# Queries, and the second half of receptances and values, as pairs of products with seven products in some chunk pairs

## The chip, the cores and the metric

The kernel runs on one core of one Trainium2 chip. The metric is the device time of one execution in microseconds, as the median of several runs. Matrix products run on TensorE (PE; its weight loads are PEld), elementwise work on VectorE (DVE), ScalarE (ACT) and GpSimd (POOL), and weights are fetched by DMA, issued from SyncE (SP).

## What is computed

One decoder layer in float32 on 256 tokens of width 2048: a feed-forward, a mixer (sliding-window attention beside an RWKV-7 recurrence, both gated), a cross attention into a memory of 256 rows, a second feed-forward, a final norm. Cut to what matters here:

```python
def gated_parallel_mixer(x, norm_g, w_in, ...):
    h = rms_norm(x, norm_g)
    p = h @ w_in                                  # 2048 x 8992
    q, k, v, p_rwkv, gates = jnp.split(p, ...)    # 1024, 256, 256, 3360, 4096 columns
    y_attn = sliding_window_attention(q, k, v, sinks)
    y_rwkv = rwkv7_time_mix(p_rwkv, ...)          # r, k, v (1024 columns each), decay, rate, gate
    gate_attn, gate_rwkv = jnp.split(jax.nn.sigmoid(gates), 2, axis=-1)
    merged = gate_attn * (y_attn @ w_proj_attn) + gate_rwkv * (y_rwkv @ w_proj_rwkv)
    return x + merged @ w_out
```

The queries are the first 1024 columns of `p`; receptances `r`, keys `k` and values `v` of the RWKV half are 1024 columns each, which the kernel takes in two halves of 512 columns, h=0 and h=1 (eight heads each).

## The kernel before

**Products.** A float32 product is made of three matmuls on numbers that were split into a high part (`hi`, rounded to TensorE's reduced float32) and the rest (`lo`): hi·hi, hi·lo, lo·hi (`times`, L470). The high part is a cast on ACT (L396), the low part a subtraction on DVE (L397). A weight comes in *units* of two chunks of 128 rows by 512 columns (half a megabyte). `weight_plan` lists all products in order, `units` and `items` are made from it, and `next_item` (L432) fetches the loads of the next units, has them split (`divide`, L408) one or two items ahead, and gives out the current one. `product` (L451) takes 16 chunks of rows, one unit at a time, for both blocks of 128 tokens: 96 matmuls for one 128x512 result each.

**Pairs with seven products.** `product_pair` (L533) computes two products with the same activations in one go, two chunks of rows by two matrices by two token blocks at a time, which is a 2x2 by 2x2 block product. A plain chunk pair takes its eight block products (24 matmuls). A chunk pair with seven takes a Strassen-like scheme of seven (21 matmuls), for which it needs four sums of weight blocks (L425 to L428), the high and low parts of those (`two_parts`, L400, names `thi` and `tlo`), and four combinations of activation blocks with their high and low parts (`combinations`, L485, lines L505 to L524). All eight PSUM banks are in use while such a chunk pair runs: `mm` and `acc` with three banks each and both banks of `tr`. The results are put together by callbacks, `first`, `middle` and `out`. Before the change only the feed-forwards use it (`gate_and_up`, `down`).

**The mixer** uses plain products. Their results leave PSUM through ACT (`scaled`, L844, scales each token by its norm factor into a tile `tok`). TensorE then transposes `tok` into features (`feat`, L654; `to_features` for queries, `shifted` for the RWKV columns). The order of products is: queries in two halves, keys with values, the small RWKV columns, RWKV keys in two halves, four attention gates alternating with `w_proj_attn`, then r and v of h=0, r and v of h=1, four RWKV gates, four of `w_proj_rwkv`, four of `w_out`, then the cross attention.

**Work beside the products** is written as generators in groups (`Interleave`): "feat" (transposes of results), "attn" (attention), "ew" (elementwise work of the recurrence: `decay_and_rate`, `removal_keys`, `substitute`, `receptances`, `values`, one at a time in this order), "chain" (`pairs(h, q)`, the recurrence itself, with many small matmuls), "norm" (`finish`, which writes the recurrence's output `yr`), "mem", and "stage". A `bg.tick()` between groups of six matmuls lets each go one step. `pairs(h, q)` waits until `substitute` and `values(h)` are done; `w_proj_rwkv` reads `yr`. `stage` prepares ten sums of weights for the second feed-forward in DRAM, starting at the items that `STAGE_AT` names. This is the order of issue in the program; the builder that turns it into the queues of the engines may move an instruction ahead of others where its inputs are there.

**Memory.** The mixer's large tiles come from one tag, `t4`, with 23 buffers of 4 KB per partition (`N4`). At its start the mixer's tiles take the place of the feed-forward's; POOL builds constants there (`mixer_constants`, L195), two of which ACT casts (L230).

## Time and profile before

| | |
|---|---|
| median of three runs | 2247.78 us (2247.43 to 2248.47) |
| the profiled execution | 2248.79 us, its span 2247.1 us |
| mean granted TensorE clock | 0.999 |
| PE busy | 2231.4 us, 99% of the span |
| PEld busy | 1833.6 us, 82% |
| DVE busy | 1820.5 us, 81% |
| ACT busy | 1245.0 us, 55% |
| POOL busy | 134.9 us, 6% |
| DMA, mean | 205 GB/s |

The profile shows one execution. Times are microseconds from the first instruction. "L397" is a line of the kernel as printed here. Busy time of PE is the union of the modelled durations of matmuls that overlap in its pipeline, so what one matmul costs is read from the distance between two starts. In a timeline a row is: start, length, engine, line, operation, output tile <- input tiles, shape, count, and in brackets the idle time before it with what ended it. In the 40 slices a digit is a busy share in tenths; a slice is 56.2 us.

### The profile page before, as it was taken

The numbers are of one execution on the slowest core, as the hardware profiler recorded it, in microseconds if no ns is written. First come the engines' busy times: TensorE is split into PE (matmuls) and PEld (weight loads), VectorE is DVE, ScalarE is ACT, GpSimd is POOL, SyncE is SP. The second block draws the span as 40 slices with busy tenths as digits, with TensorE's granted clock in tenths as the row PEclk, the third lists the DMA queues.
The fourth block names the chain that finished last, engine by engine and source line by source line (L and its number), as shares of the span: only waits on it lengthen the run. The fifth ranks groups of instructions, "written<-read, shape, count | busy, mean of one in ns | idle before, by whom it ended". The sixth has DMA issues, their size and how long they took to land.

```text
span 2247.1 us, 28239 instructions
## 1 busy us (share of the span) xinstructions
PE 2231.4 (99%) x10587; PEld 1833.6 (82%) x10587; DVE 1820.5 (81%) x2342; ACT 1245.0 (55%) x1621; POOL 134.9 (6%) x192
## 2 busy tenths in 40 slices
PE   9999999999999999999999999999999999999998
PEld 7888888888888877788888888888888888888886
DVE  7898988998989476977656666547999999999997
ACT  6555555555556567544444446456665466555654
POOL 1000000000001000201320040001000000000002
PEclk9999999999999999999999999999999999999999
DMA  7555555556556544676767576547565566556564
GB/s 264 187 201 197 201 198 202 200 188 212 195 193 201 169 135 150 198 231 207 224 214 263 187 258 227 190 167 272 197 237 204 195 231 218 201 205 221 197 229 146
DMA packets 229225, 461.35 MB, mean 205 GB/s; under 512 B 15227, under 2 KB 17504, under 8 KB 229088
## 3 DMA queue, kind: packets, MB, share of 16 engines
q1 hardware_dynamic: 220512, 433.62, 56.8%
q0 software_dynamic: 8112, 25.12, 3.5%
q8 instruction: 83, 1.36, 0.2%
q10 hardware_dynamic: 464, 0.79, 0.1%
q14 instruction: 54, 0.44, 0.1%
HBM read 435.91 MB, written 23.59 MB: 204 GB/s over the span
## 4 chain that ended last, share of the span: by engine, by line
PE 95%; DVE 2%; DMA 1%; issue 1%; ACT 1%; SPq 0%; POOL 0%; POOLq 0%; DVEq 0%; ACTq 0%
PE acc L473 19%; PE acc L474 19%; PE acc L475 19%; PE mm L475 8%; PE mm L474 8%; PE mm L473 8%; PE tr L661 2%; PE tr L474 2%; PE tr L473 2%; PE tr L475 2%; PE mm L1313 1%; DVE lo L397 1%; PE tr L1249 1%; DMA raw<-in_w_out_dram 0%; PE mm L903 0%
## 5 line engine op out<-in xcount | busy, mean ns | idle before, releaser
L396 ACT CAST hi<-raw 128x1024 fp32r<-128x1024 f32 (+1 forms) x770 | 756.5, 992 | 714.4 <-PE acc L475 514.8
L397 DVE TENSOR_TENSOR lo<-raw,hi 128x1024 fp32r<-128x1024 f32 (+1 forms) x770 | 886.1, 1153 | 315.5 <-ACT hi L396 314.0
L473 PE MATMUL acc<-hi,xhi 128*128 128x512 f32 (+1 forms) x1166 | 462.2, 397 | 2.1 <-ACT xhi L688 1.7
L474 PE MATMUL acc<-lo,xhi 128*128 128x512 f32 (+1 forms) x1166 | 452.7, 388 | 0.0
L475 PE MATMUL acc<-hi,xlo 128*128 128x512 f32 (+1 forms) x1166 | 452.5, 388 | 0.0
L473 PEld LDWEIGHTS acc<-hi,xhi 128*128 128x128 f32 x1166 | 219.4, 188 | 49.8 <-issue 4.0
L475 PEld LDWEIGHTS acc<-hi,xlo 128*128 128x128 f32 x1166 | 218.8, 188 | 46.0 <-DVE xlo L689 1.0
L474 PEld LDWEIGHTS acc<-lo,xhi 128*128 128x128 f32 x1166 | 219.2, 188 | 43.8 <-issue 1.7
L404 ACT CAST thi<-raw 128x1024 fp32r<-128x1024 f32 x192 | 199.9, 1052 | 62.9 <-DVE raw L427 42.4
L405 DVE TENSOR_TENSOR tlo<-raw,thi 128x1024 fp32r<-128x1024 f32 x192 | 232.2, 1219 | 1.1 <-ACT thi L404 0.4
L474 PE MATMUL acc<-lo,hhi 128*128 128x512 f32 x372 | 145.5, 391 | 0.8 <-DVE lo L397 0.8
L475 PE MATMUL acc<-hi,hlo 128*128 128x512 f32 x372 | 145.5, 391 | 0.0
L473 PE MATMUL mm<-hi,xhi 128*128 128x512 f32 x370 | 145.4, 393 | 0.0
L473 PE MATMUL acc<-hi,hhi 128*128 128x512 f32 x372 | 144.9, 390 | 0.0
L475 PE MATMUL mm<-hi,xlo 128*128 128x512 f32 x370 | 144.3, 390 | 0.0
L474 PE MATMUL mm<-lo,xhi 128*128 128x512 f32 x370 | 144.2, 390 | 0.0
L474 PEld LDWEIGHTS acc<-lo,hhi 128*128 128x128 f32 x372 | 69.9, 188 | 15.4 <-DVE lo L397 1.2
L473 PEld LDWEIGHTS acc<-hi,hhi 128*128 128x128 f32 x372 | 69.9, 188 | 14.3
L475 PEld LDWEIGHTS mm<-hi,xlo 128*128 128x128 f32 x370 | 69.4, 188 | 14.6
L475 PEld LDWEIGHTS acc<-hi,hlo 128*128 128x128 f32 x372 | 69.9, 188 | 14.0
L474 PEld LDWEIGHTS mm<-lo,xhi 128*128 128x128 f32 x370 | 69.5, 188 | 14.2
L473 PEld LDWEIGHTS mm<-hi,xhi 128*128 128x128 f32 x370 | 69.5, 188 | 14.0
(396 smaller groups left out, 3595.7 us busy)
## 6 DMA issues: line engine op xcount, KB each, us to landing
raw<-in_ffn_w_down_dram SPq DMA_DIRECT2D x88, 1024.0 KB, 5.1
raw<-in_ffn_w_gate_dram SPq DMA_DIRECT2D x84, 1024.0 KB, 5.1
raw<-in_ffn_w_up_dram SPq DMA_DIRECT2D x78, 1024.0 KB, 6.2
raw<-in_w_in_dram SPq DMA_DIRECT2D x136, 512.0 KB, 3.5
raw<-in_w_out_dram SPq DMA_DIRECT2D x32, 512.0 KB, 4.4
raw<-sums SPq DMA_DIRECT2D x20, 512.0 KB, 6.3
raw<-in_w_proj_attn_dram SPq DMA_DIRECT2D x16, 512.0 KB, 4.4
raw<-in_w_proj_rwkv_dram SPq DMA_DIRECT2D x16, 512.0 KB, 4.8
```

Source lines behind the costliest of these rows:

```text
L396: at["hi"] = act.copy(hi[:, s], raw[:, s])
L397: at["lo"] = dve.tensor_tensor(lo[:, s], raw[:, s], f32(hi[:, s]), ALU.subtract)
L404: act.copy(hi[:], v[:])
L405: dve.tensor_tensor(lo[:], v[:], f32(hi[:]), ALU.subtract)
L473: pe.matmul(o, xh, hi, start=first, stop=False, **how)
L474: pe.matmul(o, xh, lo, start=False, stop=False, **how)
L475: pe.matmul(o, xl, hi, start=False, stop=last, **how)
L661: pe.transpose(b[:, o : o + P], tok[:, t, col : col + P], ident[:])
L1249: pe.matmul(b[e][:, o : o + P], x1[r, j, cs_], x2[r, j, cs_], start=True, stop=True)
L1313: pe.matmul(vb[:, (o + k) * P : (o + k + 1) * P][:, r], lhs(k, e), rhs[:, k, r], start=first and k + e == 0, stop=True, **ek,)
```

## The change

The two halves of the queries become one pair of products, with seven products in chunk pairs 2, 4 and 6 of eight (counted from 0). The receptances h=1 and the values h=1 become one pair, with seven in chunk pairs 4 and 6; the order of products becomes r of h=0, v of h=0, then the pair, and `receptances(0)` is now spawned after both products of h=0. The combinations of activations are computed at the start of the mixer for pairs 2, 4 and 6 and kept for the second use. Sums of weights, their parts and the combinations take `t4` tiles there. A flag `at["sevens"]` is set from the first chunk pair with seven to the end of the last; `values` and the start of `pairs` wait while it is set. `STAGE_AT` is 16 items lower; the plan has 16 items fewer ahead of that place, since a pair of products has 8 items where two products have 16.

```diff
+SEVEN_Q, SEVEN_RV = (2, 4, 6), (4, 6)
+
-STAGE_AT = [266 + 2 * n for n in range(10)]
+STAGE_AT = [250 + 2 * n for n in range(10)]
...
-    cols = [0, 512, ATTN_W]
-    for c in cols:
-        yield w_in, 0, KD, c, 512
+    yield (w_in, w_in), 0, KD, (0, 512), SEVEN_Q
+    yield w_in, 0, KD, ATTN_W, 512
...
-    for h in range(2):
-        yield w_in, 0, KD, C_RW + h * 512, 512
-        yield w_in, 0, KD, C_RW + 2 * RW + h * 512, 512
+    for c in (C_RW, C_RW + 2 * RW):
+        yield w_in, 0, KD, c, 512
+    yield (w_in, w_in), 0, KD, (C_RW + 512, C_RW + 2 * RW + 512), SEVEN_RV
...
+    def room(name, dt=F32):
+
+        if at["pool"] is None:
+            return at["t4"](name, (P, KU, 512), dt)
+        return wp.tile([P, KU, 512], F32, tag="raw", name="raw", bufs=4)
...
     def two_parts(v, e):
         sp = at["pool"]
-        hi = sp.tile([P, KU, 512], F32R, tag="thi" + e, name="thi")
-        lo = sp.tile([P, KU, 512], F32R, tag="tlo" + e, name="tlo")
+        if sp is None:
+            hi, lo = room("thi", F32R), room("tlo", F32R)
+        else:
...
     divide:
-            t = [wp.tile([P, KU, 512], F32, tag="raw", name="raw", bufs=4) for _ in range(2)]
+            t = [room("sums") for _ in range(2)]
...
     combinations:
+                if parts:
+                    hi, lo = (p[:, o : o + n, :] for p in parts)
+                else:
+                    p = room(name, F32R)[:].rearrange("p a (b n) -> p (a b) n", n=P)
+                    hi, lo = p[:, :n], p[:, 4 : 4 + n]
...
     product_pair:
                 bg.until(lambda: c["done"] and (q > min(seven) or not bg.groups["feat"][1]))
+                at["sevens"] = True
...
                 if end:
                     middle(b)
+                    at["sevens"] = False
...
+        def scaled_pair(c, w):
+
+            s = [t4("tok", (P, 2, 512)) for _ in range(2)]
+            u = t4("u", (P, 2, 512))
+            u2, u3 = u[:, 0], u[:, 1]
+
+            def first(b):
+                act.copy(s[0][:, 0], b["p1"][:])
+                act.copy(s[1][:, 1], b["q"][:])
+
+            def middle(b):
+                dve.tensor_tensor(u2, b["p6"][:], s[0][:, 0], ALU.add)
+                dve.tensor_tensor(u3, b["p7"][:], u2, ALU.add)
+                dve.tensor_tensor(u2, b["p5"][:], u2, ALU.add)
+                dve.tensor_tensor(s[1][:, 1], s[1][:, 1], u3, ALU.add)
+
+            def out(b, to):
+                t, n = int(to in ("p4", "p5")), int(to in ("p3", "p5"))
+                o = s[n][:, t]
+                more = {"p2": o, "p4": u3, "p3": u2, "p5": o}[to]
+                dve.tensor_tensor(o, b[to][:], more, ALU.add)
+                act.activation(o, o, AF.Copy, scale=n2.r[t])
+
+            product_pair(n2.x, c, w, first, middle, out)
+            return s
...
+        cx = combinations(None, n2.x, SEVEN_Q, "c", early=False)
         qt = []
-        for h in range(2):
-            tok = scaled(product(n2.x, W["w_in"]), n2.r)
+        for tok in scaled_pair(cx, W["w_in"]):
             qt.append(t4("qt"))
-            bg.spawn("feat", to_features(tok, qt[h], "q"))
+            bg.spawn("feat", to_features(tok, qt[-1], "q"))
...
     values (twice), and pairs after its idle steps:
+                while at["sevens"]:
+                    yield
...
         for h in range(2):
             rt.append(t4("rt"))
-            columns4(rt[h], 4 * h, f"r{h}")
+            if h == 0:
+                columns4(rt[h], 4 * h, f"r{h}")
+                bv.append(t4("bv"))
+                columns4(bv[h], 16 + 4 * h, f"v{h}")
+            else:
+                bv.append(t4("bv"))
+                for tok, o, m, name in zip(scaled_pair(cx, W["w_in"]), (rt[h], bv[h]), (4, 20), "rv"):
+                    bg.spawn("feat", shifted(
+                        tok, C4, [m + i for i in range(4)], [o[:, i, :] for i in range(4)],
+                        name + "1",
+                    ))
             bg.spawn("ew", receptances(h))
-            bv.append(t4("bv"))
-            columns4(bv[h], 16 + 4 * h, f"v{h}")
             bg.spawn("ew", values(h))
```

More of the change, by code (lines that the diff above doesn't have):

```diff
@@ L319, in decoder_layer @@
             continue
+        if len(ends) == 1:
+            for q in range(nk // KU):
+                items.append(((len(units), len(units) + 1), q in n))
+                units += [(v, k0 + KU * q, c, 512) for v, c in zip(w, c0)]
+            continue
         for k in range(k0, k0 + nk, 2 * KU):
@@ L330, in decoder_layer @@
     sums_d = dram.tile([len(staged), P, 4, 512], F32, name="sums")
-    at = {"item": 0, "product": 0, "pool": None}
+    at = {"item": 0, "product": 0, "pool": None, "sevens": False}
+    def room(name, dt=F32):
+        if at["pool"] is None:
+            return at["t4"](name, (P, KU, 512), dt)
+        return wp.tile([P, KU, 512], F32, tag="raw", name="raw", bufs=4)
     def load(u, pieces=None):
@@ L401, in two_parts @@
         sp = at["pool"]
-        hi = sp.tile([P, KU, 512], F32R, tag="thi" + e, name="thi")
-        lo = sp.tile([P, KU, 512], F32R, tag="tlo" + e, name="tlo")
+        if sp is None:
+            hi, lo = room("thi", F32R), room("tlo", F32R)
+        else:
+            hi = sp.tile([P, KU, 512], F32R, tag="thi" + e, name="thi")
+            lo = sp.tile([P, KU, 512], F32R, tag="tlo" + e, name="tlo")
         act.copy(hi[:], v[:])
@@ L490, in combinations @@
         n = n or sum(4 if q in seven else 2 for q in pairs)
-        parts = [sp.tile([P, n, P], F32R, tag=name + e, name=name + e) for e in ("hi", "lo")]
-        c = {"parts": parts, "at": {}, "done": False, "seven": seven, "early": early}
+        parts = sp and [
+            sp.tile([P, n, P], F32R, tag=name + e, name=name + e) for e in ("hi", "lo")
+        ]
+        c = {"at": {}, "done": False, "seven": seven, "early": early}
         def work():
@@ L500, in work @@
                     yield
-                t = wp.tile([P, KU, 512], F32, tag="raw", name="raw", bufs=4)
+                t = room("sums")
                 v = t[:, 0].rearrange("p (k t n) -> p k t n", k=2, t=2)
@@ L518, in work @@
                 yield
[L519 removed]
+                if parts:
[3 more added lines that the diff above has]
+                    hi, lo = p[:, :n], p[:, 4 : 4 + n]
                 with tc.issue_after(at["hi"].ins):
[L521 removed]
+                    act.copy(hi, f[:, :n])
                 yield
                 with tc.issue_after(at["lo"].ins):
[L524 to L525 removed]
+                    dve.tensor_tensor(lo, f[:, :n], f32(hi), ALU.subtract)
+                c["at"][q] = hi, lo
                 o += n
@@ L556, in of_c @@
         def of_c(q, i):
-            return [p[:, c["at"][q] + i, :] for p in c["parts"]]
+            return [p[:, i, :] for p in c["at"][q]]
         def of_w(parts_, i):
@@ L1207, in values @@
             for i in (0, 2):
+                while at["sevens"]:
+                    yield
                 b = head_sums(
@@ L1271, in pairs @@
             yield from idle(4 + 4 * q)
+            while at["sevens"]:
+                yield
             ah, bh, kh, rh = at_[h], bt[h], aa[h], rt[h]
```

5 lines of the change are left out of this document (1 added, 4 removed).

## The prediction

> **What bounds the kernel now.** I read the page first (engine line, slices), then the windows over the stretches that the change rewrites, the waits, and last the timelines of PE and DVE there.
>
> ```profile
> span 2247.1 us, 28239 instructions
> ...
> PE 2231.4 (99%) x10587; PEld 1833.6 (82%) x10587; DVE 1820.5 (81%) x2342; ACT 1245.0 (55%) x1621; POOL 134.9 (6%) x192
> ...
> DVE  7898988998989476977656666547999999999997
> ```
>
> PE is the bound: 2231.4 us of 2247.1. DVE stands at eight or nine tenths in the two feed-forwards and falls to four to seven, with a single nine, in slices 14 to 28, where the mixer and the cross attention lie. That gap is what the change spends. The windows put numbers on it: a piece of the feed-forward's end, then the two halves of the queries, then the second receptances and the second values (columns: length, busy time and count of PE, weight load, DVE, ACT, POOL, then granted clock).
>
> ```profile
> 660.00:680.00 20.00, 20.00 (x89) 16.26 (x88) 19.82 (x24) 11.23 (x13) 0.00 (x0) 1.00 0.53 178
> 715.00:738.00 23.00, 23.00 (x111) 19.10 (x110) 15.71 (x23) 14.46 (x27) 6.60 (x25) 1.00 0.65 208
> 738.00:761.00 23.00, 23.00 (x107) 19.05 (x106) 10.09 (x9) 11.05 (x13) 0.00 (x0) 1.00 0.63 197
> ...
> 1063.00:1086.00 23.00, 23.00 (x107) 19.03 (x106) 11.39 (x12) 10.96 (x13) 2.31 (x4) 1.00 0.60 186
> 1086.00:1118.00 32.00, 31.49 (x177) 25.99 (x176) 23.07 (x29) 15.05 (x19) 15.67 (x22) 1.00 0.74 234
> ```
>
> PE is full in all of them. In the feed-forward, where pairs of seven products are in use already, DVE works 19.82 of 20 us and PE still does not wait: seven products in three of eight pairs is just what DVE can carry there. In the queries DVE works 25.8 of 46 us, in the receptances and values 34.5 of 55.
>
> **What is saved.** A chunk pair costs eight products of three matmuls each, or seven. Three pairs of the queries and two of the second half drop one product: 5 x 3 = 15 matmuls. Their price is the distance from start to start, not the 390 ns that one lasts:
>
> ```profile
> 715.28 0.39 PE L473 MATMUL acc<-hi,xhi 128*128 128x512 f32 x1
> ...
> 721.43 1.03 PE L661 MATMUL tr<-ident,x 128*128 128x128 f32 x8
> ...
> 727.34 0.39 PE L473 MATMUL acc<-hi,xhi 128*128 128x512 f32 x1
> ...
> 734.14 0.39 PE L473 MATMUL acc<-hi,xhi 128*128 128x512 f32 x1
> ```
>
> From 727.34 to 734.14 there are 30 starts, 0.227 us each. So 15 matmuls are 3.40 us: 2.04 in the queries, 1.36 in the second half. This is 0.15% of the time, and no other PE work goes: the transposes are the same, and the same 32 half-megabyte units of weights are fetched in another order, so DMA is left at nothing.
>
> **What is added on DVE.** The costs stand in the feed-forward's own pair of seven:
>
> ```profile
> 699.70 0.68 DVE L425 TENSOR_TENSOR raw<-raw,raw 128x512 f32<-128x512 f32 x1
> 700.30 0.68 DVE L426 TENSOR_TENSOR raw<-raw 128x512 f32<-128x512 f32 x1
> 700.90 0.68 DVE L427 TENSOR_TENSOR raw<-raw,raw 128x512 f32<-128x512 f32 x1
> 701.50 1.22 DVE L397 TENSOR_TENSOR lo<-raw,hi 128x1024 fp32r<-128x1024 f32 x1
> 702.64 0.68 DVE L428 TENSOR_TENSOR raw<-raw,raw 128x512 f32<-128x512 f32 x1
> 703.24 1.22 DVE L405 TENSOR_TENSOR tlo<-raw,thi 128x1024 fp32r<-128x1024 f32 x1
> 704.38 0.68 DVE L397 TENSOR_TENSOR lo<-raw,hi 128x512 fp32r<-128x512 f32 x1
> 704.98 1.22 DVE L405 TENSOR_TENSOR tlo<-raw,thi 128x1024 fp32r<-128x1024 f32 x1
> ```
>
> Start to start, a sum of weights takes 0.60, a full low part 1.14, a half one 0.60. A seven-pair is 4 x 0.60 + 1.14 + 0.60 + 2 x 1.14 = 6.42 us; a plain pair is two low parts, 2.28. Each seven-pair adds 4.14 us. The combinations of the activations:
>
> ```profile
> 655.10 0.68 DVE L505 TENSOR_TENSOR raw<-hhi,hlo 128x512 f32<-128x512 f32 x1
> 655.70 0.68 DVE L667 TENSOR_TENSOR hlo<-tr,hhi 128x512 fp32r<-128x512 f32 x1
> 656.30 0.28 DVE L511 TENSOR_TENSOR raw<-raw 128x128 f32<-128x128 f32 x1
> 656.50 0.28 DVE L513 TENSOR_TENSOR raw<-raw 128x128 f32<-128x128 f32 x1
> ...
> 658.91 0.68 DVE L524 TENSOR_TENSOR dlo<-raw,dhi 128x512 fp32r<-128x512 f32 x1
> 659.51 0.68 DVE L428 TENSOR_TENSOR raw<-raw,raw 128x512 f32<-128x512 f32 x1
> ```
>
> 0.60 + 4 x 0.20 + 0.60 = 2.0 us a pair, three pairs, in the queries alone (the second half reuses two of them). The end of a product pair, which was four scalings on ACT, gets four sums and four additions of a 128x512 tile on DVE, 8 x 0.60 = 4.8 us each time. ACT gets 1.5 more casts of about 1 us in each seven-pair; with 14.46 of 23 us and 11.05 of 23 busy it has room, so I cost that at nothing, covered by PE (without the cover: 1.6 us a pair).
>
> **The queries.** DVE's work there becomes 25.8 + 3 x 4.14 + 6.0 + 4.8 = 49.0 us, and PE needs only 46 - 2.0 = 44.0. Up to 2.4 us (the four last additions) can run behind PE's end, so DVE is 2.6 to 5.0 us short even if it never stands. And the work is not spread evenly:
>
> ```profile
> 715.71 1.28 DVE L634 SCALAR_TENSOR_TENSOR x<-acc,x 128x512 f32<-128x512 f32 x2
> ...
> 721.34 1.22 DVE L397 TENSOR_TENSOR lo<-raw,hi 128x1024 fp32r<-128x1024 f32 x1
> ...
> 726.26 0.17 DVE L708 TENSOR_SCALAR ms<-ms 128x2 f32<-128x2 f32 x1
> 727.00 1.23 DVE L397 TENSOR_TENSOR lo<-raw,hi 128x1024 fp32r<-128x1024 f32 x1 [0.57 <-ACT hi L396]
> 731.78 2.36 DVE L397 TENSOR_TENSOR lo<-raw,hi 128x1024 fp32r<-128x1024 f32 x2 [3.55 <-ACT hi L396]
> ```
>
> Up to 726.4 DVE still closes the feed-forward and the norm. PE has by then begun the pair of queries at 715.28; two plain pairs (48 matmuls, 10.9 us) and 16 transposes (0.1 us each by the row above) bring it to the first seven-pair at 727.8. DVE fills its small gaps with the first combination's sums (1.4 us), then has before PE can start: its low part 0.6, the next combination's sums 1.4, the weight sums 2.4, and a cast. That is 726.4 + 4.4 = 730.8, plus ACT's cast of about 1: PE waits 3 to 3.5 us at the first seven-pair. Behind it stand the other combinations (2.6 us) and two low parts ahead of the next plain pair: another 1.5 to 2 us. Later pairs then find DVE in step. Both ways give about 5; below stands 2.6 (work alone), above 7.5 if ACT's casts come late as well. No gain can come from here, since no DVE instruction goes away. I take 5.0. The pair of queries so ends about 3.0 us later than now.
>
> **The second half.** The receptances h=1 and values h=1 become one pair, two seven-pairs of which come late (fifth and seventh). DVE gets 2 x 4.14 + 4.8 = 13.1 us more on 34.5 of 55, and has room on the whole; but in the four chunk pairs where the two fall, PE takes 2 x 24 + 2 x 21 = 90 matmuls, 20.4 us, and DVE needs 2 x 6.42 + 2 x 2.28 = 17.4, beside 1.2 of the keys' low part and one or two staging sums (2.4 us each), which start 16 items earlier by number and about as far in the work. Stall from 0 to 1.5 us; I take 0.7, nearer to the feed-forward's row (99% busy, no wait). Net -0.7.
>
> While a pair of seven holds all PSUM banks, the values' transposes and the chain wait (the new checks on "sevens"). Two steps of `values(0)` and so `pairs(0, ...)` move from inside values h=1 to the first gate product, about seven ticks of six matmuls later, 7 x 6 x 0.227 = 9.5 us of PE work. Who waits: the last rows of the RWKV output.
>
> ```profile
> L667 DVE TENSOR_TENSOR yrlo<-yq,yrhi x4: 683/689/693, 1184.6 to 1273.8; 128x512 fp32r<-128x512 f32 x4
> ...
> L475 PE MATMUL acc<-hi,yrlo x64: 389/389/398, 1294.9 to 1340.6; 128*128 128x512 f32 x64
> ```
>
> The last part is ready at 1274.5 and first read at 1294: 20 us of cover, so the delay costs nothing; beyond 20 us each us would be PE's.
>
> **The sum**, on the profiled execution (2248.79 us, of which 2247.1 is span): -3.40 + 5.0 + 0.7 = +2.3, 2251.1. The median of the three runs is 1.0 lower than that execution, so I forecast 2250.1 us. Its own range, with the bounds above (2.6 to 7.5 and 0 to 1.5), is 2247.0 to 2253.4.
>
> **Rivals.** (1) *DVE keeps up.* The builder's order can put combinations and sums into gaps that I count as lost, as the feed-forward shows at 99%. Then only the saving is left: 2247.8 - 3.4 = 2244.4. Against it: 49 us of DVE work in 44. To be faster by over 0.2% (4.5 us) takes 1.1 us beyond the saving; the mixer's remaining PE idle, 0.5 us in 1086 to 1118, does not hold that.
>
> (2) *ACT blocks the first seven-pair.* The constants' casts wait for POOL:
>
> ```profile
> 726.09 0.31 POOL L198 MEMSET abias<- 128x256 f32 x1 [6.89 <-ACT junk L697]
> ...
> 730.29 0.30 ACT L230 CAST ones_r<-bdones 128x128 fp32r<-128x128 f32 x1 [3.32 <-POOL bdones L221]
> ```
>
> POOL cannot start before the norm has left the old buffer, and ACT stands 3.3 us for it; DVE's 3.55 us of idle time at 731.78 is the same wait. Today the ready weights hide it. If these two casts stay ahead of the combination's and the sums' casts, DVE loses its 3.3 us inside a stretch where it has none to lose: 5.0 becomes 8.3, and the time 2253.4, slower. It decides once DVE's backlog at 727 is over nothing, and by the walk above it is.
>
> (3) *The chain comes too late.* Two or three more `t4` tiles are held from the queries on, and each seven-pair takes six of the 23; if keys and values queue for them over 20 us in all, PE stands ahead of `w_proj_rwkv`. With 6 us beyond the cover: about 2256. For it: the delay of 9.5 us uses half of the cover.
>
> (4) *One long wait slows the clock.* If the stall at the first seven-pair is one piece, PE could come back at half rate for as long again: 3.4 us at twice 0.227 a matmul lose 1.7 us, 2251.8. The windows here show a clock of 1.00 throughout, and no wait of that length to test it. The Trainium skill, "TensorE: Matmul & The Clock Gate", Part 1, has such a rule: after an idle window of about 3.4 us the array runs at half its clock.
>
> **How the numbers follow.** Forecast 0.43, DVE keeps up 0.20, ACT blocks 0.26, late chain 0.08, clock 0.03. About 0.2% (4.5 us) is what a measurement of this kernel can tell from no change: 2243.3 to 2252.3. Slower by more: 0.07 of the forecast's own upper end, 0.22 of ACT's 0.26, 0.07 of the late chain's, 0.36. Faster by more: 0.06, from the first rival with something that I do not see. The rest, 0.58, is within. The range, 2244.0 to 2257.0, reaches from the first rival's time to the late chain's; about 0.06 lie under it and 0.1 above.
>
> **What would show it.** In the changed kernel's waits, PE `tr` or `acc` at L474/L473 should wait some 5 us on DVE (`tlo`, `lo`, the combinations) between 725 and 760, DVE should be 95% busy or more in that window, and the first kv product should end about 3 us later. PE without a wait there, with the product 2 us earlier, is the first rival; ACT's L230 with over 3 us idle and `thi` behind it, the second; PE waiting at `yrhi` or `yrlo`, the third; a granted clock below 0.95 there, the fourth. I am wrong altogether if the time moves outside these two stretches.

## The result, and the profile after

The changed kernel takes 2258.56 us (2257.97 to 2259.24, four runs); the kernel before takes 2247.7 us in the same measurement. The ratio is 1.0047, interval [1.0035, 1.006]: slower by 10.9 us, and above the forecast of 2250.1 and the upper end of its range. The profiled execution took 2259.24 us, its span is 2257.5. Lines of the code have moved by the change: the casts of weights are L408 (before L396), the low parts L409 (L397), the two constants' casts L231 (L230), the matmuls L488 to L490 (L473 to L475). New names: `sums` at L440 to L443 are the sums of weights, `thi` and `tlo` at L419 and L420 their parts, `c` at L542 and L545 the parts of the combinations. The edits of the experiments move these numbers by a few lines more.

The page's engine line after:

```profile
PE 2234.7 (99%) x10572; PEld 1833.5 (81%) x10572; DVE 1856.5 (82%) x2406; ACT 1255.3 (56%) x1638; POOL 136.5 (6%) x192
```

The 15 matmuls are gone (10587 to 10572), DVE has 36 us more work, and the share of PE still reads 99%. The page does not show where 10 us went; two tiles tell it. `vt` is copied out of PSUM when the keys-and-values product ends, the first product after the queries. `gl` is the first use of `w_proj_rwkv`, after all of the second half. Before, then after (the tiles' rows: shortest/median/longest ns, first and last start):

```profile
L889 ACT ACTIVATE vt<-acc,rs x2: 466/468/471, 783.8 to 785.1; 128x256 f32<-128x256 f32 x2
L1459 DVE TENSOR_TENSOR gl<-acc,gl x8: 679/681/683, 1305.1 to 1341.3; 128x512 f32<-128x512 f32 x8
```

```profile
L939 ACT ACTIVATE vt<-acc,rs x2: 464/466/467, 794.5 to 795.9; 128x256 f32<-128x256 f32 x2
L1523 DVE TENSOR_TENSOR gl<-acc,gl x8: 679/680/684, 1316.4 to 1352.6; 128x512 f32<-128x512 f32 x8
```

The queries begin at the same time in both (715.3 and 715.5), so 10.7 us are lost by the end of the first product behind them, and 11.3 by `gl`: the loss lies in the queries, although nine matmuls were saved there. The windows of after over the queries, which answer to the two shown of before (length; busy time and count of PE, weight load, DVE, ACT, POOL; granted clock; DMA):

```profile
715.00:738.00 23.00, 18.62 (x81) 14.24 (x80) 18.83 (x36) 13.35 (x27) 7.51 (x25) 0.87 0.38 124
738.00:761.00 23.00, 21.07 (x81) 16.07 (x80) 18.55 (x26) 10.53 (x13) 0.00 (x0) 0.90 0.52 178
```

PE, full before, now has 18.62 of 23 us and then 21.07. DVE was forecast at 95% or more and has only 82% and 81%: it was not simply short of time, it stood still as well. And the clock column reads 0.87 and 0.90 where it read 1.00. The waits of PE in this part, then those of ACT (us in total, times, the longest):

```profile
PE acc L488 <- ACT hi L408: 3.2, 1, 3.2
PE tr L488 <- ACT thi L419: 2.9, 3, 1.2
```

```profile
ACT thi L419 <- DVE sums L442: 6.5, 3, 4.4
ACT ones_r L231 <- POOL bdones L222: 4.7, 1, 4.7
```

Read together they are one chain. POOL holds ACT for 4.7 us at the constants' casts. The cast `hi` of the weights stands right behind them (731.80), and PE's longest wait, 3.2 us, ends with it. DVE's `c` waits 3.1 us for the cast behind that one; the next sums come late, and `thi` and PE's waits at `tr` follow those. The timelines of ACT and DVE show the order, with the idle time in brackets:

```profile
731.40 0.30 ACT L231 CAST ones_r<-bdones 128x128 fp32r<-128x128 f32 x1 [4.67 <-POOL bdones L222]
731.60 0.29 ACT L231 CAST ones_r<-bdmean 128x128 fp32r<-128x128 f32 x1
731.80 1.04 ACT L408 CAST hi<-raw 128x1024 fp32r<-128x1024 f32 x1
732.75 0.61 ACT L542 CAST c<-sums 128x512 fp32r<-128x512 f32 x1
...
736.13 1.04 ACT L419 CAST thi<-sums 128x1024 fp32r<-128x1024 f32 x1 [1.82 <-DVE sums L442]
```

```profile
729.65 0.68 DVE L440 TENSOR_TENSOR sums<-raw 128x512 f32<-128x512 f32 x1
733.40 0.69 DVE L545 TENSOR_TENSOR c<-sums,c 128x512 fp32r<-128x512 f32 x1 [3.06 <-ACT c L542]
...
757.25 0.69 DVE L440 TENSOR_TENSOR sums<-raw 128x512 f32<-128x512 f32 x1 [2.00 <-DMA raw<-in_w_in_dram]
```

And PE's timeline there:

```profile
729.35 0.39 PE L490 MATMUL acc<-hi,xlo 128*128 128x512 f32 x1
732.90 0.80 PE L488 MATMUL acc<-hi,xhi 128*128 128x512 f32 x1 [3.16 <-ACT hi L408]
...
735.38 0.63 PE L488 MATMUL mm<-hi,xhi 128*128 128x512 f32 x1
737.23 1.22 PE L488 MATMUL tr<-thi,c 128*128 128x512 f32 x2 [1.22 <-ACT thi L419]
738.25 0.63 PE L489 MATMUL acc<-lo,xhi 128*128 128x512 f32 x1
738.68 0.63 PE L490 MATMUL acc<-hi,xlo 128*128 128x512 f32 x1
```

From 738.25 to 738.68 two starts lie 0.43 us apart, nearly twice the 0.227 of before. Taking each distance between starts against 0.227 gives the loss in its parts: the two gaps at 729.35 and 735.38 lose 3.32 and 1.62 us; the matmuls between and behind them until 742.4, at half clock, 3.9; the second and third pair with seven 3.5 (at 750.3 0.72, at 758.8 1.26 behind the late weights of the row at 757.25, the rest in pieces). That is 12.3 of the 12.7 us that are to be explained (10.7 lost and 2.04 saved).

### The profile page after: what moved, and what is told of

The parts are those of the page before. It is cut to its first block, busy times and chain, and to the rows that moved or that the text cites. A ratio compares the mean times of both kernels' runs of the same rounds, so it can differ in the third digit from the quotient of the medians.

```text
span 2257.5 us, 28305 instructions
## 1 busy us (share of the span) xinstructions
PE 2234.7 (99%) x10572; PEld 1833.5 (81%) x10572; DVE 1856.5 (82%) x2406; ACT 1255.3 (56%) x1638; POOL 136.5 (6%) x192
## 3 DMA queue, kind: packets, MB, share of 16 engines
q8 instruction: 83, 1.36, 0.2%
## 4 chain that ended last, share of the span: by engine, by line
PE 91%; DVE 4%; issue 2%; DMA 1%; ACT 1%; POOL 0%; SPq 0%; POOLq 0%; ACTq 0%; DVEq 0%
PE acc L488 18%; PE acc L489 18%; PE acc L490 18%; PE mm L489 8%; PE mm L490 8%; PE mm L488 8%; PE tr L684 2%; PE tr L489 2%; PE tr L488 2%; PE tr L490 2%; DVE lo L409 2%; PE mm L1369 1%; PE tr L1303 1%; DMA raw<-in_w_in_dram 1%; PE mm L953 0%
## 5 line engine op out<-in xcount | busy, mean ns | idle before, releaser
L408 ACT CAST hi<-raw 128x1024 fp32r<-128x1024 f32 (+1 forms) x770 | 753.9, 989 | 706.4 <-PE acc L490 498.7
L409 DVE TENSOR_TENSOR lo<-raw,hi 128x1024 fp32r<-128x1024 f32 (+1 forms) x770 | 883.2, 1150 | 283.6 <-ACT hi L408 281.9
L488 PE MATMUL acc<-hi,xhi 128*128 128x512 f32 (+1 forms) x1105 | 439.3, 398 | 5.2 <-ACT hi L408 3.2
L489 PE MATMUL acc<-lo,xhi 128*128 128x512 f32 (+1 forms) x1105 | 430.5, 390 | 0.0
L490 PE MATMUL acc<-hi,xlo 128*128 128x512 f32 (+1 forms) x1105 | 429.9, 389 | 0.0
L488 PEld LDWEIGHTS acc<-hi,xhi 128*128 128x128 f32 x1105 | 208.6, 189 | 51.8 <-ACT hi L408 4.0
L490 PEld LDWEIGHTS acc<-hi,xlo 128*128 128x128 f32 x1105 | 208.0, 188 | 42.9 <-issue 0.3
L489 PEld LDWEIGHTS acc<-lo,xhi 128*128 128x128 f32 x1105 | 208.5, 189 | 41.9 <-issue 1.7
L420 DVE TENSOR_TENSOR tlo<-raw,thi 128x1024 fp32r<-128x1024 f32 x192 | 231.8, 1217 | 1.3 <-ACT thi L419 0.4
L419 ACT CAST thi<-raw 128x1024 fp32r<-128x1024 f32 x192 | 199.7, 1051 | 59.6 <-DVE raw L442 38.9
L488 PE MATMUL mm<-hi,xhi 128*128 128x512 f32 x401 | 157.9, 394 | 0.3 <-ACT hi L408 0.3
L490 PE MATMUL mm<-hi,xlo 128*128 128x512 f32 x401 | 156.3, 390 | 0.0
L489 PE MATMUL mm<-lo,xhi 128*128 128x512 f32 x401 | 156.3, 390 | 0.0
L490 PE MATMUL acc<-hi,hlo 128*128 128x512 f32 x372 | 145.5, 391 | 0.0
L488 PE MATMUL acc<-hi,hhi 128*128 128x512 f32 x372 | 145.0, 390 | 0.0
L488 PEld LDWEIGHTS mm<-hi,xhi 128*128 128x128 f32 x401 | 75.5, 188 | 16.0 <-ACT hi L408 0.7
L490 PEld LDWEIGHTS mm<-hi,xlo 128*128 128x128 f32 x401 | 75.3, 188 | 15.9
L488 PEld LDWEIGHTS acc<-hi,hhi 128*128 128x128 f32 x372 | 69.8, 188 | 14.4
L490 PEld LDWEIGHTS acc<-hi,hlo 128*128 128x128 f32 x372 | 69.9, 188 | 14.1
```

The lines of the kernel that those rows point to most:

```text
L408: at["hi"] = act.copy(hi[:, s], raw[:, s])
L409: at["lo"] = dve.tensor_tensor(lo[:, s], raw[:, s], f32(hi[:, s]), ALU.subtract)
L419: act.copy(hi[:], v[:])
L420: dve.tensor_tensor(lo[:], v[:], f32(hi[:]), ALU.subtract)
L488: pe.matmul(o, xh, hi, start=first, stop=False, **how)
L489: pe.matmul(o, xh, lo, start=False, stop=False, **how)
```

## The experiments

Four causes stand in that chain: DVE short of time (the forecast), ACT held by POOL (the second rival), the clock (the fourth), and late weights (not foreseen). The runs were made to tell them apart.

**Half of the change alone.** In queries_plain the second half is changed alone; the queries are two plain products again (the combinations of two chunk pairs, which the second half needs, are still built at the mixer's start, and `STAGE_AT` follows the plan):

```diff
-    yield (w_in, w_in), 0, KD, (0, 512), SEVEN_Q
-    yield w_in, 0, KD, ATTN_W, 512
+    for c in (0, 512, ATTN_W):
+        yield w_in, 0, KD, c, 512
...
-        for tok in scaled_pair(cx, W["w_in"]):
+        for h in range(2):
+            tok = scaled(product(n2.x, W["w_in"]), n2.r)
```

> The changed kernel with the queries as two plain products again (the combinations of two pairs, which the second half needs, still built at the mixer's start). Theory (all of the loss lies in the queries; the second half saves 1.4 us and gives it back): 2247.5 to 2248.5, and the queries as long as before. Rival (the second half costs too, by the chain's delay or by the tiles): over 2250.

Measured: 2249.38 us beside 2249.19 of the kernel before in the same measurement, ratio 1.0001 [0.9991, 1.001]. The theory's 2247.5 to 2248.5 is level with the 2247.7 that the kernel before took in the first measurement; here too the two are level. In rv_plain the queries are changed alone:

```diff
-    for c in (C_RW, C_RW + 2 * RW):
-        yield w_in, 0, KD, c, 512
-    yield (w_in, w_in), 0, KD, (C_RW + 512, C_RW + 2 * RW + 512), SEVEN_RV
+    for h in range(2):
+        yield w_in, 0, KD, C_RW + h * 512, 512
+        yield w_in, 0, KD, C_RW + 2 * RW + h * 512, 512
```

> The changed kernel with receptances and values of h=1 as two plain products again. Theory (the loss lies in the queries): 2257.5 to 2259, as the changed kernel. Rival (the second half costs): 2255 or less.

Measured: 2257.73 us, ratio 1.0037 [1.0024, 1.005], as the theory has it. The tiles' rows of the first and of the second:

```profile
L940 ACT ACTIVATE vt<-acc,rs x2: 464/466/467, 784.0 to 785.4; 128x256 f32<-128x256 f32 x2
L1524 DVE TENSOR_TENSOR gl<-acc,gl x8: 681/681/684, 1305.6 to 1341.8; 128x512 f32<-128x512 f32 x8
```

```profile
L939 ACT ACTIVATE vt<-acc,rs x2: 464/466/467, 792.8 to 794.1; 128x256 f32<-128x256 f32 x2
L1515 DVE TENSOR_TENSOR gl<-acc,gl x8: 679/681/683, 1314.5 to 1350.7; 128x512 f32<-128x512 f32 x8
```

The queries alone lose 9.0 us before `vt` and nearly nothing after it; the second half alone is at `gl` 0.5 us late, 0.2 of it from before `vt`. The loss is the queries', and the second half neither earns its 1.36 us nor costs more than about 0.3.

Up to `vt` rv_plain runs the same code as the changed kernel, and still its `vt` comes 1.7 us earlier. The two gaps of PE at the first pair with seven are as long in both (3.32 and 1.62 us), but the half clock lasts 6.83 us and not 10.24, so the slow starts cost 3.0 us and not 3.9, and the stalls at the later pairs cost 2.9 and not 3.5. A difference at `vt` between two single traces is uncertain by about that much.

**ACT's stop.** In casts_late the two constants' casts are issued behind the pair of queries:

```diff
-            act.copy(r[:], v[:])
-            ones_r.append(r)
+            ones_r.append((r, v))
...
+        with tc.issue_after(at["hi"].ins):
+            for r_, v_ in late_r:
+                act.copy(r_[:], v_[:])
```

> The changed kernel, with the two ACT casts of the block-diagonal constants issued behind the pair of queries instead of ahead of its first seven-pair. Theory (ACT stood 4.7 us for POOL there, PE stood over 3 us behind it, and the clock then fell to half for some 25 matmuls): the wait of 3.2 us at the first seven-pair and the clock of 0.5 both go; what is left is DVE's shortage of 2 to 5 us, so 2249 to 2252 against 2258.6. Rival (DVE is simply short of time in the queries): PE waits as long, now on DVE, and no more than 3 us are gained, 2255.5 or more.

Measured: 2256.34 us beside 2249.19 of the kernel before, ratio 1.0031 [1.0019, 1.0043], and `vt` at 790.4, 4.1 us earlier than in the changed kernel and 2.4 earlier than in rv_plain. The time itself lies in the rival's interval; the loss is 7.2 us where it was 10.9, and the two intervals of the ratio overlap a little. ACT's stop is gone from this stretch, but half and more of the expected gain did not come. What took its place (the first window, then a short one, then the row of PE's waits):

```profile
715.00:738.00 23.00, 20.24 (x89) 15.69 (x88) 21.90 (x38) 14.99 (x27) 7.72 (x25) 0.94 0.53 168
```

```profile
734.00:738.00 4.00, 3.83 (x11) 3.03 (x12) 4.00 (x5) 2.28 (x4) 0.00 (x0) 0.67 0.93 294
```

```profile
PE tr L487 <- ACT thi L418: 3.9, 3, 2.5
```

DVE is now at 21.90 of 23 us, 95%, and full at the first pair with seven; PE waits 2.5 us there for the sums and their parts, and the clock still falls. In the next 23 us DVE is at 19.61, 85%, and waits 1.7 us for weights. So ACT's stop is a cause, for 2.4 to 4.1 us at `vt` with the clock time that hung on it, and behind it stands the forecast's own cause.

**The clock.** In keep_warm eight small matmuls of constants are put ahead of the first pair with seven, so that PE has something to do in its gap:

```diff
+                if at["pool"] is None and q == 2:
+                    idle_ = mm()
+                    for _ in range(8):
+                        pe.matmul(idle_[:, :P], ones[:], ones[:], start=True, stop=True)
```

> The changed kernel, with eight matmuls of ones (128x128, float32, into an unused PSUM bank, result not read) between the second plain pair of the queries and the first seven-pair, where PE stands. Theory (the wait itself is 3.3 us and the slow clock behind it costs about 5 us more): the wait stays about as long in sum but is filled, the clock stays at 1.00 from 730 to 743, and 4 to 5.5 us are gained, about 2253.5. Rival (the clock in the records costs nothing, the slow matmuls wait for their operands): time unchanged or up to 1 us more, 2258 to 2260.

Measured: 2258.88 us, ratio 1.0041 [1.0026, 1.0056]. It failed: they ran at 727.8 to 729.5, ahead of the gap and not in it, and the clock fell all the same, at 734.4 instead of 732.1. To price the clock by itself, wait_short and wait_long give the kernel before a wait between the two halves of its queries and change nothing else: a matmul, and behind it the second half, that wait for a row of POOL operations, two (K = 1) and five (K = 4).

```diff
-            tok = scaled(product(n2.x, W["w_in"]), n2.r)
+            with tc.issue_after(hold_pe.ins) if h else nullcontext():
+                tok = scaled(product(n2.x, W["w_in"]), n2.r)
...
+            if h == 0:
+                slow = t4("slow", (P, 2, 512))
+                pool.tensor_tensor(slow[:, 0], tok[:, 0, :], tok[:, 1, :], ALU.add)
+                for i in range(K):
+                    pool.tensor_tensor(slow[:, 0], slow[:, 0], slow[:, 0], ALU.subtract)
+                bank = mm()
+                hold_pe = pe.matmul(bank[:, :P], slow[:, 0, :P], ones[:], start=True, stop=True)
```

> The kernel before, with a made wait on PE between the two halves of the queries: two GpSimd operations of about 1 us each on the first half's result, a small matmul that reads them (result not read), and the second half's matmuls behind it. PE stands 2.5 to 3.5 us. Theory (the clock falls after PE has stood for about as long as the 3.3 us seen): the clock stays at 1.00 or falls for a few matmuls only; lost is about the wait. Rival (any wait of over 2 us halves the clock for some 25 matmuls): another 5 us lost.

> As wait_short with five GpSimd operations, so PE stands 5.5 to 7 us. Theory: the clock falls to half and stays there for several microseconds after PE works again; start to start 0.43 us instead of 0.227 for 10 to 25 matmuls, so 2 to 5 us are lost beyond the wait. Rival (a halved clock only shows where the matmuls wait for operands anyway): the matmuls behind the wait start 0.227 us apart.

Measured in one execution each: 2255.07 and 2257.74 us. PE's starts leave 4.26 us and 7.62 us empty, and `vt` comes 6.7 and 9.7 us late (790.5 and 793.5 beside 783.8). The shorter wait so costs 2.4 us beyond itself, the longer one 2.1: a price that doesn't grow with the wait. For wait_short neither side came true (the clock fell, but 2.4 us were lost beyond the wait and not 5); for wait_long the theory did. Windows, with their edges laid where the clock changes, show why; wait_short, then wait_long:

```profile
737.58:740.99 3.41, 1.40 (x7) 0.82 (x5) 1.35 (x2) 2.31 (x3) 1.20 (x1) 1.00 0.76 232
740.99:744.40 3.41, 1.32 (x4) 1.22 (x5) 1.14 (x1) 0.00 (x0) 1.96 (x2) 0.50 0.51 142
744.40:747.81 3.41, 3.41 (x11) 2.72 (x11) 0.00 (x0) 0.48 (x1) 0.00 (x0) 0.50 0.23 88
```

```profile
736.80:740.21 3.41, 2.08 (x10) 1.38 (x8) 1.23 (x1) 2.44 (x4) 0.53 (x1) 1.00 0.79 238
740.21:743.62 3.41, 0.00 (x0) 0.00 (x0) 1.46 (x1) 0.33 (x1) 3.25 (x3) 1.00 0.52 148
743.62:747.03 3.41, 0.69 (x3) 0.69 (x4) 0.00 (x0) 0.00 (x0) 2.51 (x3) 0.50 0.39 139
747.03:750.44 3.41, 3.41 (x12) 2.72 (x12) 0.00 (x0) 0.00 (x0) 0.00 (x0) 0.50 0.00 0
```

The clock knows two values, 1.00 and 0.50, and stays at half for two times 3.41 us in both. In the longer one it did not fall during the first 3.41 us that hold a part of the wait (10 matmuls ran in them), but after the stretch with none. What the slow matmuls cost is set by how much of these 6.83 us lies behind the wait, 4.7 and 4.1 us, and not by the wait's length.

**The order of products.** In kv_first the keys and values come ahead of the pair of queries; kv_first_late has the casts of the constants behind the pair as well:

```diff
+    yield w_in, 0, KD, ATTN_W, 512
     yield (w_in, w_in), 0, KD, (0, 512), SEVEN_Q
-    yield w_in, 0, KD, ATTN_W, 512
```

> As kv_first_late, but with the constants' casts left where they are. Theory (a stop of 4 to 5 us on ACT hurts only where the weights are needed at once): with plain products behind it, PE waits 0 to 1 us more than in kv_first_late. Rival (the stop costs PE wherever it is): 3 us more.

> The changed kernel with the plain product for keys and values in front of the pair of queries, and the constants' casts behind that pair. The combinations, the norm's end and the constants then lie under 22 us of plain matmuls. Theory (the queries lose because DVE has the norm's end, the combinations and three seven-pairs in one stretch, and because ACT stands there): no PE wait over 0.5 us and no slow clock in the queries, which then save their 2 us; the second half gives nothing, so about 2 us under the kernel before, ratio 0.999. Rival (three seven-pairs of eight are too many for DVE and for four weight buffers also without the combinations): PE still waits 3 us or more in the queries, ratio 1.001 or more.

Measured: 2255.08 us, ratio 1.0029 [1.0017, 1.0041], and 2253.52 us, ratio 1.0024 [1.0015, 1.0033]. Neither is faster than the kernel before, though 2 us were forecast for kv_first_late. DVE is done with the feed-forward and the norm when the first pair with seven comes, and the stretch that was at 18.62, where the plain product now lies, is full again, at full clock (kv_first_late, the window and DVE's longest waits between 735 and 790):

```profile
715.00:738.00 23.00, 23.00 (x111) 19.11 (x110) 21.73 (x40) 15.85 (x28) 9.31 (x25) 1.00 0.68 206
```

```profile
DVE sums L439 <- DMA raw<-in_w_in_dram: 7.3, 3, 3.8
```

But DVE now stands 7.3 us for weights in the 55 us of the pair. A mixer's unit lives in a ring `raw` of four buffers, the units of two chunk pairs; a pair with seven keeps its four blocks until the last sum, so that the loads behind it can only start late (the feed-forward has a ring of its own, `raw2`, with twice the depth). PE lost about 1.5 us in this stretch (21.99 of 23 and 23.52 of 24 us in the two windows behind the one shown), yet `gl` starts at 1308.8, 3.7 us late. Waits that the kernel before doesn't have stand behind the queries: 1.5 us at the attention's transposes (`tr`, L998, three times, for DVE), and 1.7 us for `hi` and 0.5 for `lo` between 976 and 980, at the first product with `w_proj_attn`. Why this order brings them was not tried. kv_first takes 1.6 us more than kv_first_late, between its theory's 0 to 1 and its rival's 3: PE waits 2.6 us from 715 to 790 and not 1.4, and behind the same wait near 980 its clock falls for one stretch of 3.41 us, from 982.6, which it does not in kv_first_late.

**Late weights.** In deep, which is casts_late otherwise, the weights of the queries' pairs with seven are fetched into `t4` tiles, eight units ahead:

```diff
+        elif u in roomy and at["pool"] is None:
+            raw = at["t4"]("rawt", (P, KU, n))
...
-        for v in range(u, u + (2 * LOADED if at["pool"] is not None else LOADED)):
+        for v in range(u, u + (2 * LOADED if at["pool"] is not None or i < Q_END else LOADED)):
```

> As casts_late (the two constants' casts behind the query pair), and the weights of the queries' seven-pairs are fetched into tiles of the mixer's own pool, up to eight units ahead and not four, so that DVE's weight sums and ACT's casts need not wait for a transfer. Theory (part of the rest is DVE standing for weights that a ring of four buffers fetches late): DVE's waits on raw weights in the queries go, 1 to 2.5 us gained on casts_late's 2256.3, so 2254 to 2255.5, ratio 1.0022 to 1.003. Rival (DVE is simply short of time and would wait later for want of it): no gain, 2256, ratio 1.003 or over.

Measured: 2253.36 us, ratio 1.0021 [1.0012, 1.003]. The interval overlaps that of casts_late; beside its own kernel before the loss is 4.6 us where it was 7.2, and in the profile `vt` comes at 787.7, 2.7 us earlier than there. DVE waits for no transfer any more in this stretch, and it is busy for 44.3 of 46 us (21.92 and 22.38 of 23). 3.9 us are still lost at `vt`, 5.9 with the 2.04 that the matmuls save. Of these 1.6 are slow starts in a half-rate stretch, since PE starts only 5 matmuls in the 3.4 us ahead of it:

```profile
730.10:733.50 3.40, 2.06 (x5) 1.04 (x6) 3.40 (x7) 3.12 (x4) 1.66 (x9) 1.00 0.44 168
733.50:736.90 3.40, 3.40 (x9) 2.34 (x8) 3.39 (x3) 2.52 (x3) 0.00 (x0) 0.50 0.63 187
```

About 4.3 us remain, with DVE full. PE's waits there end on ACT's casts of weights:

```profile
PE mm L492 <- ACT hi L412: 1.5, 3, 1.0
```

These stand in ACT's order behind a cast that waits 2.1 us for DVE's sums and one that waits 1.1 us for a transfer. If all but the transfer is DVE's, its extra work costs 3.2 us by itself, and at most 4.3; no run takes the two apart. The forecast's term for it was 5.0, between 2.6 and 7.5.

The first pair with seven waits, in all these kernels, until all three combinations are issued. deep_each is deep, with a wait for its own combination only:

```diff
-                bg.until(lambda: c["done"] and (q > min(seven) or not bg.groups["feat"][1]))
+                bg.until(lambda: q in c["at"] and (q > min(seven) or not bg.groups["feat"][1]))
```

> As deep, and each seven-pair of the queries waits for its own combination of the activations alone, not for all three, so that 2.6 us of DVE work (the other two combinations) need not stand ahead of the first one's weight sums. Theory (PE's remaining wait of 2.7 us at the first seven-pair is that DVE work in line, and it trips the clock): the wait falls under 1.5 us, the clock stays at 1.00, and 3 to 5 us are gained on deep: 2250 to 2252, ratio 1.0005 to 1.0015. Rival (the work only moves behind the first pair, DVE being short in sum): under 1.5 us gained, 2253 or more, ratio over 1.002.

Measured: 2253.62 us, ratio 1.0022 [1.0013, 1.003]: nothing gained on deep. The theory that this order was at fault falls. The third combination did move behind the first pair (its sums now start at 737.96), DVE stayed full, and the clock fell as before:

```profile
729.32:732.73 3.41, 1.53 (x4) 0.56 (x3) 3.41 (x8) 2.94 (x4) 2.43 (x15) 1.00 0.66 255
732.73:736.14 3.41, 3.21 (x7) 2.25 (x8) 3.02 (x4) 2.58 (x4) 0.00 (x0) 0.50 0.44 118
```

**One pair fewer.** q46 is the changed kernel with two pairs of seven in the queries, the fifth and the seventh. No other line is changed, but one combination (2.0 us of DVE's work) goes with the third pair, and the first pair with seven now comes two chunk pairs later, so that this run can't tell fewer from later:

```diff
-SEVEN_Q, SEVEN_RV = (2, 4, 6), (4, 6)
+SEVEN_Q, SEVEN_RV = (4, 6), (4, 6)
```

> As the changed kernel, but the queries use seven products in two of eight chunk pairs (the fifth and the seventh), not three: one size changed. Saved in the queries 6 matmuls x 0.227 = 1.36 us. Theory (the first seven-pair comes too early, where DVE still closes the norm and ACT stands for POOL, and DVE is short of time): DVE has 6.1 us less to do, 42.9 us in the 44.7 that PE needs, and four plain pairs (22 us) cover the start, so no wait of 3 us and no fall of the clock; 2247 to 2249.5, ratio 0.9985 to 1.001. Rival (each seven-pair of the mixer costs its 3 to 4 us by the shallow ring of weight buffers and the order of DVE's work, wherever it stands): two thirds of the 10.9 us stay, 2255, ratio 1.003.

Measured: 2250.86 us, ratio 1.0011 [1.0002, 1.002], a little above the theory's interval and far below the rival's. The clock stays at 1.00, and `vt` starts at 786.2: 8.3 of the 10.7 us are gone with one pair of seven. ACT stands 4.2 us for POOL as ever. The ready weights of the plain pairs keep PE at work over it, but DVE idles 2.64 us behind the same stop and is full from there on, and PE waits 1.8 us at the first pair with seven, from 739 to 741.7. DVE's wait for late weights comes behind that, up to 747, and costs PE 0.8 us at the second pair (a window, and DVE's rows):

```profile
738.00:742.00 4.00, 2.20 (x9) 1.27 (x8) 4.00 (x6) 3.06 (x4) 0.00 (x0) 1.00 0.39 120
```

```profile
732.56 1.23 DVE L409 TENSOR_TENSOR lo<-raw,hi 128x1024 fp32r<-128x1024 f32 x1 [2.64 <-ACT hi L408]
...
746.96 0.69 DVE L440 TENSOR_TENSOR sums<-raw 128x512 f32<-128x512 f32 x1 [2.47 <-DMA raw<-in_w_in_dram]
```

That leaves ACT's stop, by way of DVE, and the late weights. The last kernel, q46_deep, takes q46 and deep together, and so both away at once:

> As deep, but the queries use seven products in the fifth and the seventh pair only, as in q46: the version with every cause found so far taken out. Theory (the loss of the changed kernel was the early seven-pair, the stop of ACT, the clock that fell behind it, and late weights): PE waits under 1 us in the queries, the first kv product ends within 1 us of the kernel before, and the time is 2246.5 to 2249 beside 2248.5 of the kernel before, ratio 0.999 to 1.0005. Rival (PE waits come from DVE's order of work at each seven-pair, not from late weights): 2250 to 2251, as q46, ratio 1.001.

Measured: 2248.88 us beside 2249.07 of the kernel before, ratio 1.0001 [0.9992, 1.001], as the theory has it. PE's waits in the queries come to 0.8 us in all, and the first product behind them ends 0.6 us earlier than before:

```profile
PE tr L492 <- ACT thi L423: 0.8, 1, 0.8
```

```profile
L949 ACT ACTIVATE vt<-acc,rs x2: 464/466/467, 783.2 to 784.6; 128x256 f32<-128x256 f32 x2
L1533 DVE TENSOR_TENSOR gl<-acc,gl x8: 679/682/684, 1305.1 to 1341.3; 128x512 f32<-128x512 f32 x8
```

With every cause found taken out, and 12 matmuls (2.7 us) saved, the kernel is level with the one before. No version ran faster than it.

## Why the prediction was wrong

**The saving** was right: 15 matmuls are gone, and where PE doesn't wait its starts stay 0.227 us apart.

**The place** was right in part: all of the loss lies where the stall of 5.0 us was put, at the pairs with seven of the queries, and most of it at the first one, forecast at 727.8; PE's last matmul before the gap starts at 729.35. One sum in that walk is off: 730.8 and a cast of 1 us make 731.8, which is 4.0 us behind 727.8 and not 3 to 3.5. That is small beside what was missed.

**The term that failed is the stall, "I take 5.0"**: it measured 12.7 us (10.7 lost, 2.04 saved). Taken apart by the traces on the way to deep, the 12.7 are 4.1 for ACT's stop with its clock time, 2.7 for late weights, 1.6 for the slow clock that is left, and a rest of 4.3, each uncertain by the 1.7 us that two traces of the same code differ. The rest, which holds the DVE shortage (3.2 to 4.3 us), lies within the forecast's bounds, but three more terms lie on top. Two were priced at nothing, "ACT ... I cost that at nothing, covered by PE" and "DMA is left at nothing". The third was in a rival with 0.03.

**ACT at nothing** is the first step that failed. The second rival had seen the stop (3.3 us before, 4.7 after), the place and the mechanism: the constants' casts did stay ahead of the combination's, and DVE's backlog made it count. The share of busy time, 14.46 of 23 us, was the wrong argument for the cover: for 4.67 us ACT did nothing, and the cast that PE needed came right behind the one that waited. Taking that stop away gained 2.4 to 4.1 us at `vt` (beside rv_plain and beside the changed kernel), against the 3.3 of the rival's price; a part of that is the slow clock, which lasted one stretch of 3.41 us in casts_late, two in rv_plain and three in the changed kernel.

**The clock at 0.03** is the second. The prediction had no wait of that length to test it, and took one long wait as the condition and 1.7 us as the price. The runs show the condition to be weaker, a stretch of 3.41 us with few matmuls. It was met in the changed kernel (5 matmuls ran in the stretch ahead of the fall), and again in the two stretches behind, with 6 matmuls each, so the half clock lasted 10.2 us and its slow starts cost 3.9. These two rivals do not exclude each other, as a sum of chances over single cases supposes: ACT's stop makes the gap, and the gap makes the slow clock. The prices add up to 2250.1 + 3.3 + 1.7 = 2255.1 by the prediction's own numbers, inside its range but with no chance of its own.

**DMA at nothing** is the third; it cost 2.7 us at `vt` (deep against casts_late). The bytes were the same, as the text said; what changed is how long a buffer is held. This is the part that no line of the trace before could show, since `raw` in the mixer had no pair of seven, and the feed-forward's pairs use another ring. The name `raw` and its four buffers stood in the code.

**"DVE 95% busy"** was wrong for the changed kernel, 82%. With ACT's stop out it was 95% in the first 23 us and 85% in the next (casts_late), and 96% over both only with the late weights out too (deep). An engine can be short of time and stand idle in the same window when its inputs are late.

**The second half** was forecast at -0.7 us, a saving of 1.36 less a stall of 0.7, and gave +0.3 at `gl` in the run with that half alone (+0.2 in time, within noise). The saving was lost, but not where the forecast put its stall: PE waits for no weights in that pair. From the starts of all matmuls between the values of h=0 and `gl`, the run of large matmuls behind large ones is 1.6 us shorter, as the saving says; hand-overs from large to small ones (51 of them) take 1.05 us longer in sum and the small ones among themselves 0.85. So the saving is given back by the recurrence's own matmuls. PE's waits in its transposes (`mk`, `bv`) are 0.6 us of that, 1.1 in place of 0.5; why the rest became slower was not tried and stays open.

**The chain** was right: the last part of the recurrence's output was forecast to come 9.5 us later beside the rest, within a cover of 20. Its last row now starts at 1296.7 (before 1273.8), with the first use moved 11.3 us: 11.6 us of the cover used, about 9 left, and PE does not wait for it:

```profile
L490 PE MATMUL acc<-hi,yrlo x64: 389/389/398, 1306.2 to 1352.0; 128*128 128x512 f32 x64
L690 DVE TENSOR_TENSOR yrlo<-yq,yrhi x4: 681/684/691, 1205.3 to 1296.7; 128x512 fp32r<-128x512 f32 x4
```

## What to carry to other kernels

A wait that costs nothing today is priced by the work that is ready behind it; a change that makes more work pass through the engine that stands there (here ACT, for POOL, under two pairs of weights) should be charged the whole wait, and the cover should be counted in ready instructions and not in shares of busy time. Look up how many buffers stand behind each tile name on the new path and how long the new step holds one: with the same bytes moved, a ring of four became the limit where a pair of seven holds its blocks to the end. When two rivals share a cause, give their sum a chance of its own, and try a smaller dose first: two pairs of seven instead of three, the first of them later, took away 8.3 of 10.7 us. Where single traces are compared, look for two runs of the same code first: here they differed by 1.7 us.

## What the runs showed of the hardware

The granted clock of TensorE had two values only, and within the program its low stretches came in multiples of one length: 3.41 us (casts_late, deep, deep_each, kv_first), 6.83 (both waits, keep_warm, rv_plain) and 10.24 (the changed kernel). At half clock the starts of 512-column matmuls were 0.427 us apart, at full clock 0.227. The Trainium skill, "TensorE: Matmul & The Clock Gate", Part 1, states a free-running window of 3413 ns and two clocks, and these runs agree with both. The grid of such stretches runs through the whole program: the changed kernel's clock falls at 8.52, at 732.14 and, when the program ends, at 2251.07, which lie 212.0 and 445.0 times 3.4133 us apart, and in all 14 traces every edge fits its trace's grid in this way. Where the grid lies against the program differs from trace to trace.

The Trainium skill, in the same part, speaks of an idle window as what brings the clock down. Here a stretch need not be idle: those in which 0, 2, 4, 5, 5, 5, 6, 7 and 7 matmuls ran (wait_long, rv_plain, deep_each, deep, casts_late, the changed kernel, keep_warm, wait_short and kv_first; the count in the windows' PE column) were followed by the half clock, those with 8 (kv_first_late, 975.01 to 978.42) and 10 (wait_long) were not. At half clock, stretches with 3, 4, 5 and 6 matmuls were followed by another at half, those with 7 to 12 by the full clock. Laid over all 14 traces, the grid gives one limit: at full clock every stretch with 7 matmuls or fewer was followed by the half clock (23 of them, 10 with none), and of some 9,000 others only three were, in the first 9 us, where most matmuls are small. At full clock 15 starts would fit in a stretch. No run was made to try this limit.

q46 shows what the grid does. From 738.5 to 741.9 only 6 matmuls run, and the clock stays up: its grid, counted back from the fall at the program's end (2245.36, 441 stretches later), has an edge at 740.08, which cuts the gap in two.

```profile
736.67:740.08 3.41, 2.90 (x13) 2.07 (x12) 3.41 (x6) 2.58 (x4) 0.00 (x0) 1.00 0.57 171
740.08:743.49 3.41, 2.11 (x9) 1.52 (x9) 3.41 (x5) 2.26 (x3) 0.00 (x0) 1.00 0.50 147
```

So whether one gap costs the clock depends on where the grid happens to lie, and that q46's clock stayed up is in part luck.
